# A two-layer diffusion trunk on one core: a new order for the opening's small products, and layer 1's spectrum products held in program order

## The chip, the core and the metric

The kernel runs on one NeuronCore of a Trainium2 chip. The metric is the device time of one execution in microseconds (us). Five engines work side by side, each with its own instruction stream: TensorE multiplies matrices (PE in the profile, PEld for its weight loads), VectorE (DVE) and ScalarE (ACT) work element by element, GpSimd (POOL) does a few small operations, and SyncE's queue (SP) issues the transfers from memory. Engines wait for one another through semaphores.

## The reference

Two layers (DEPTH = 2) over 256 context tokens and 256 latent tokens of width 1024. Each layer normalises, modulates with a vector that comes from `c` and `c_ctx` through `w_mod`, projects with `w_in`, runs four mixers (attention, a Hyena long convolution, pooling, gated MLP), gates and merges them, and ends with a SwiGLU block:

```python
mod = (act_lat @ w_mod[l] + b_mod[l])[:, None, :]
sh1, s1, g1, sh2, s2, g2 = jnp.split(mod, 6, axis=-1)
p = modulate(x, norm1_w[l], sh1, s1) @ w_in[l]      # rms_norm(x) * (1 + s1) + sh1
x = x + g1 * parallel_mixers(p, attn, lp)
x = x + g2 * swiglu(modulate(x, norm2_w[l], sh2, s2), ...)
```

The Hyena mixer needs filters that come from a small sine network (three layers of `sin(freq * (h @ w + b))`) and their spectra, which the kernel computes as products with a DFT matrix. All of it is float32.

## The kernel before

Everything is kept with features on the partitions: x is eight tiles of 128 features by 512 tokens. A weight unit of 128x1024 is fetched by SP, rounded to `whi` (ScalarE) and its remainder `wlo` (VectorE); activations are split the same way (`hh`, `hl`), and each product is three matmuls, hi·hi, hi·lo and lo·hi (`mm3`).

**The opening** (lines 654 to 758) stands inside `tc.manual_schedule()`: there each engine runs its instructions in the order in which the code writes them. It does the following.

- Eight tiles of x come in, then the weights of the modulation in four "chunks" (`w_mod`, eight transfers each), with a unit of `w_wide` behind each chunk.
- `dense(n)` issues products of ones that nobody reads, into the bank `warm`.
- The sums of squares: ScalarE squares each tile of x (line 678), and a product ones x squares adds it into all 128 rows of a bank (line 686, two records each in the profile, as float32 takes two passes). Tiles 4 to 7 are first added in pairs on VectorE (line 685).
- The diagonal of that bank is read by four reductions on VectorE (line 690), GpSimd raises it to the power -0.5 (line 695), `rstd_diag` spreads it over a diagonal (line 350, tile `dg`), and `rstd_spread` makes `rb`, the factor in all rows, by one product with ones (line 360).
- `chunk_mods(8)` multiplies one chunk (line 283, 64 records); its tail on VectorE is a transpose (line 294), additions (line 299) and the factor `amod` (line 304). Group g of two tiles of x needs chunk g.
- Four groups g = 0 to 3 follow. Each normalises tiles 2g and 2g+1 (`norm_tiles`: `nt` at line 382 begins the group, `hh` and `hl` of the first tile, then line 378, 389, 391 and 405 for the second), multiplies the first tile (`next(w0)`, line 728, twelve matmuls), does a step of the sine network, multiplies chunk g+1, and multiplies the second tile (twelve matmuls).
- `mlp` is the sine network, a generator in seven steps. Step 1 is the first product and three VectorE operations ("A", lines 414 to 417), step 2 the range reduction ("B", four operations, lines 420 to 422), step 3 the sine on ScalarE (line 424), the second product (line 434) and its A, step 4 its B, step 5 sine, third product and A, step 6 B, step 7 the last sine. Before, steps 1 and 2 stand ahead of the sums, step 3 within them, and steps 4 to 7 in the groups 0 to 3, each between the first tile's product and the next chunk's.

**After the opening** a planner orders each engine's instructions by what its own model says is ready; a wait on the chip follows from that order. `tc.keep_in_program_order(r)` binds an instruction behind the one that the code wrote just before it on its engine.

**The end of layer 0** is such a planned place. The last residual gives sums of squares, by columns: `sums_of` (line 322) multiplies 128 token columns of the squares, as weights, with one column of ones, four products (eight records, line 328) for a tile. `rstd` (one VectorE operation, line 337, and GpSimd's power, line 339) and `rstd_bcast` (lines 350 and 360) follow, and then layer 1's first tile. The code writes layer 1's spectrum products (`spectrum_mm`, five of six matmuls each, B0, B1, A0, A1, C0) around this chain: B0 behind the first `sums_of`, B1 and A0 behind the second, A1 and C0 behind the product that makes `rb`. The same pattern stands in the middle of layer 0 with the four filter products of layer 1 (`filter_mm`, line 474): the first behind the first `sums_of`, the second behind the chain's start, the third behind `rb`.

Of the kernel before, what the change touches and what calls it, by code (L numbers as in the profile page):

```python
# [11 lines left out]
F32 = mybir.dt.float32  # L12
# [3 lines left out]
ALU = mybir.AluOpType  # L16
AX = mybir.AxisListType

P = 128
D = 1024  # L20
KT = D // P
# [9 lines left out]
EPS = 1e-6  # L31
# [71 lines left out]
def trunk_kernel(ctx: ExitStack, tc: tile.TileContext, I, out: bass.AP):  # L103
# [32 lines left out]
    def load_const(name, shape):  # L136
        t = const(name, shape)
        SY.dma_start(out=t, in_=I[name])
        return t

    def split(hi, lo, src):
        S.copy(hi, src)
        V.tensor_sub(lo, src, f32(hi))
# [63 lines left out]
            split_next()  # L207
        flush()

    def mm3(o, wh, wl, xh, xl, first, last):  # L210
        T.matmul(o, lhsT=wh, rhs=xh, start=first, stop=False)  # L211
        T.matmul(o, lhsT=wh, rhs=xl, start=False, stop=False)  # L212
        T.matmul(o, lhsT=wl, rhs=xh, start=False, stop=last)  # L213


    pa = load_const("pack_a", [P, 280])
# [254 lines left out]
    def filter_mm(l, p, o):  # L471
        w3, _, f = flt[l]
        f[p, o] = side("pf")
        T.matmul(f[p, o], lhsT=hk[:, p * P : p * P + P], rhs=w3[o], start=True, stop=True)

    def filter_keep(l, p, o):

# [74 lines left out]
    def spectrum_mm(l, name, parts, fwd, nyq):  # L552

        k, col, mat = {
            "A0": (0, 0, fwd), "A1": (0, 128, fwd), "B0": (1, 0, nyq), "B1": (1, 384, fwd), "C0": (0, 128, nyq)
        }[name]
        o = side("sp")
        for p in range(2):
            h, lo = mat[p]
            mm3(o, h[:, col : col + P], lo[:, col : col + P], *parts[k][p], p == 0, p == 1)  # L560
        spectra.setdefault(l, {})[name] = o

    def spectrum_out(l, name, skip):
# [87 lines left out]
        return vec  # L651


    start = [True]
    opened = ExitStack()
    opened.enter_context(tc.manual_schedule())
    x = fresh_x()
# [6 lines left out]
    wide = t2(s="wide")  # L664
    V.memset(wide, 1.0)

    def dense(n):

        for _ in range(n):
            T.matmul(warm, lhsT=ones, rhs=wide, start=True, stop=True)  # L670

    dense(2)
    next(mlp)
# [2 lines left out]
    for j in range(KT):  # L676
        sq = t2(s="sq")
        S.activation(sq, x[j], AF.Square)
        if j == 3:
            next(mlp)  # L680
        if j in (4, 6):
            held = sq
            continue
        if j in (5, 7):
            V.tensor_add(sq, held, sq)
        T.matmul(tot, lhsT=ones, rhs=sq, start=(j == 0), stop=(j == KT - 1))
    r = small([P, 4], F32, "rs")
    for t in range(4):
        sl = slice(t * P, t * P + P)
        V.tensor_tensor_reduce(  # L690
            out=junk[:, :P], in0=tot[:, sl], in1=ident, scale=1.0 / D, scalar=EPS,
            op0=ALU.mult, op1=ALU.add, accum_out=r[:, t : t + 1],
        )
    r2 = small([P, 4], F32, "rs")
    G.tensor_tensor(r2, r, halfexp[:, :4], op=ALU.pow)
    dense(1)
    dg = rstd_diag(r2, 0, NTOK)
    chunk_mods(KT)
    rb = rstd_spread(dg, 0, NTOK)
    chunk_load(2)  # L700
    rest = []
    split_next(rest)
# [1 line left out]
    for l in range(DEPTH):  # L704
# [9 lines left out]
        def wide_gen(w, tset, ncols):  # L714
            os_ = {t: bank("w") for t in tset}
            for u in range(4):
                hi, lo = unit("w_wide", l, w, u)
                for k in range(2):
                    kt = 2 * u + k
                    hh, hl = hs[kt]  # L720
                    terms = [(hh, hi), (hh, lo), (hl, hi)]
                    ts = [(t, i) for t in tset for i in range(3)]
                    if start and kt % 2 == 0:
                        ts.sort(key=lambda v: v[1])
                    for t, i in ts:
                        n = ncols(t)
                        a, b = terms[i]
                        T.matmul(  # L728
                            os_[t][:, :n], lhsT=a[:, t * P : t * P + P], rhs=b[:, k * 512 : k * 512 + n],
                            start=(kt == 0 and i == 0), stop=(kt == 7 and i == 2),  # L730
                        )
                    if k:
                        done()
                    yield os_

        w0 = wide_gen(0, range(4), lambda t: 512 if t in tts else 256)
        if l == 0:
            def between(after):
                if not after and rest:
                    rest.pop(0)()  # L740

            for g in range(4):
                if g == 0:
                    chunk_load(3)
                if g:
                    split_next(rest)
                if g == 3:
                    SY.dma_start(out=pb[:, 646:], in_=I["pack_b"][:, 646:])
                    vec = vec_load(0)
                    silu_rows()  # L750
                hs += norm_tiles(l, 0, x, rb, 0, NTOK, range(2 * g, 2 * g + 2), between)
                if g == 3:
                    count["look"] = LOOK
                os_ = next(w0)
                next(mlp, None)
                chunk_mods(KT)
                os_ = next(w0)
            opened.close()
            start.clear()
        else:  # L760
            for i, h in enumerate(norm_tiles(l, 0, x, rb, 0, NTOK, range(KT))):
                hs.append(h)
                os_ = next(w0)
                if i in (2, 3, 4):
                    spectrum_out(1, ("A0", "A1", "C0")[i - 2], flt[1][3])
# [820 lines left out]
```

## Time and profile before

| what | value |
|---|---|
| time, median of 3 runs | 1321.97 us (1321.88 to 1325.45) |
| the profiled execution: its time | 1321.89 us |
| the profiled execution: its span, first to last instruction | 1320.1 us |
| matmuls of the span | 7694, TensorE busy 1293.7 us |
| mean granted TensorE clock | 0.997 of full speed |

1.79 us of the profiled time lie outside the span. Times in the rows are microseconds from the span's start. In a timeline row the columns are start, duration, engine, line, operation, tiles written and read, how many instructions were merged, and in brackets the idle time before them and what ended it.

### The profile page before, as it was taken

The numbers are of one execution on the slowest core, as the hardware profiler recorded it, in microseconds if no ns is written. First come the engines' busy times: TensorE is split into PE (matmuls) and PEld (weight loads), VectorE is DVE, ScalarE is ACT, GpSimd is POOL, SyncE is SP. The second block draws the span as 40 slices with busy tenths as digits, with TensorE's granted clock in tenths as the row PEclk, the third lists the DMA queues.
The fourth block names the chain that finished last, engine by engine and source line by source line (L and its number), as shares of the span: only waits on it lengthen the run. The fifth ranks groups of instructions, "written<-read, shape, count | busy, mean of one in ns | idle before, by whom it ended". The sixth has DMA issues, their size and how long they took to land.

```text
span 1320.1 us, 19990 instructions
## 1 busy us (share of the span) xinstructions
PE 1293.7 (98%) x7694; PEld 1121.6 (85%) x7694; DVE 936.7 (71%) x1615; ACT 607.6 (46%) x1059; POOL 64.1 (5%) x69
## 2 busy tenths in 40 slices
PE   8999999999999999999999999999999999999997
PEld 4778788888888878888888887889989999999997
DVE  5785896998977455677667677865889876655554
ACT  4652333377743336222122224365458854643443
POOL 0102300300000000000000000002110000000000
PEclk9999999999999999999999999999999999999999
DMA  9732234433445452554555553424434457565551
GB/s 352 284 100 92 88 120 139 134 127 105 131 137 170 157 184 97 159 176 159 170 168 178 186 176 128 159 80 129 140 106 139 151 191 251 160 185 183 184 185 48
DMA packets 68351, 204.90 MB, mean 155 GB/s; under 512 B 7584, under 2 KB 13856, under 8 KB 68128
## 3 DMA queue, kind: packets, MB, share of 16 engines
q1 hardware_dynamic: 68256, 203.63, 47.4%
q8 instruction: 60, 0.98, 0.3%
q14 instruction: 35, 0.29, 0.1%
HBM read 202.55 MB, written 1.05 MB: 154 GB/s over the span
## 4 chain that ended last, share of the span: by engine, by line
PE 72%; issue 17%; DVE 7%; ACT 2%; POOL 1%; DMA 0%; DVEq 0%; POOLq 0%; ACTq 0%
PE pmn L211 14%; PE pmn L213 14%; PE pmn L212 14%; PE pmw L728 4%; PE pmd L213 3%; PE pmd L212 3%; PE pmd L211 3%; PE pmb L211 2%; PE pmb L213 2%; PE pmb L212 2%; DVE wlo L176 2%; PE psav L1246 1%; PE pspt L1224 1%; PE pmk L211 1%; PE pmk L212 1%
## 5 line engine op out<-in xcount | busy, mean ns | idle before, releaser
L173 ACT CAST whi<-raw 128x1024 fp32r<-128x1024 f32 (+2 forms) x316 | 288.4, 920 | 476.2 <-PE pmn L212 221.0
L211 PE MATMUL pmn<-hh,whi 128*128 128x512 f32 (+1 forms) x1328 | 450.5, 339 | 0.6 <-DVE vst L777 0.6
L212 PE MATMUL pmn<-hl,whi 128*128 128x512 f32 (+1 forms) x1328 | 447.8, 337 | 0.0
L213 PE MATMUL pmn<-hh,wlo 128*128 128x512 f32 (+1 forms) x1328 | 446.7, 336 | 0.3 <-DVE wlo L176 0.3
L176 DVE TENSOR_TENSOR wlo<-raw,whi 128x1024 fp32r<-128x1024 f32 (+2 forms) x316 | 336.3, 1067 | 148.5 <-ACT whi L173 146.1
L211 PEld LDWEIGHTS pmn<-hh,whi 128*128 128x128 f32 x1328 | 251.9, 190 | 28.1 <-issue 1.1
L213 PEld LDWEIGHTS pmn<-hh,wlo 128*128 128x128 f32 x1328 | 251.8, 190 | 26.9 <-DVE wlo L176 0.7
L212 PEld LDWEIGHTS pmn<-hl,whi 128*128 128x128 f32 x1328 | 252.0, 190 | 26.5 <-issue 1.2
L253 DVE CUSTOM_DVE_ANT_0 junk<-raw,cb,pack_a 128x1024 bf16<-128x1024 f32 x144 | 187.1, 1299 | 1.4
L211 PE MATMUL pmd<-hh,whi 128*128 128x512 f32 (+1 forms) x352 | 118.8, 337 | 0.0
L212 PE MATMUL pmd<-hl,whi 128*128 128x512 f32 (+1 forms) x352 | 118.7, 337 | 0.0
L213 PE MATMUL pmd<-hh,wlo 128*128 128x512 f32 (+1 forms) x352 | 118.4, 337 | 0.0
L213 PEld LDWEIGHTS pmd<-hh,wlo 128*128 128x128 f32 x352 | 66.8, 190 | 7.2 <-issue 0.5
L212 PEld LDWEIGHTS pmd<-hl,whi 128*128 128x128 f32 x352 | 66.8, 190 | 7.1 <-issue 0.2
L211 PEld LDWEIGHTS pmd<-hh,whi 128*128 128x128 f32 x352 | 66.8, 190 | 7.1 <-issue 0.2
L1372 DVE TENSOR_TENSOR sg<-sg,pmn 128x512 f32<-128x512 f32 (+1 forms) x42 | 23.3, 554 | 64.9 <-PE pmn L213 64.9
L339 POOL TENSOR_TENSOR rs<-rs,halfexp 128x4 f32<-128x4 f32 (+1 forms) x4 | 3.4, 852 | 939.3 <-DVE rs L337 939.3
L728 PE MATMUL pmw<-whi,hh 128*128 128x512 f32 (+1 forms) x112 | 41.2, 386 | 2.5 <-ACT hh L385 1.4
L728 PE MATMUL pmw<-wlo,hh 128*128 128x512 f32 (+1 forms) x112 | 40.1, 376 | 0.0
L728 PE MATMUL pmw<-whi,hl 128*128 128x512 f32 (+1 forms) x112 | 39.9, 377 | 0.0
L1300 DVE SCALAR_TENSOR_TENSOR x<-pmd,mod,x 128x256 f32<-128x256 f32 x48 | 21.8, 478 | 24.5 <-PE pmd L213 24.5
L1209 ACT ACTIVATE pe<-pssc,mx 128x512 f32<-128x512 f32 (+1 forms) x48 | 29.6, 618 | 16.6 <-DVE mx L1206 16.5
(284 smaller groups left out, 1868.3 us busy)
## 6 DMA issues: line engine op xcount, KB each, us to landing
raw<-in_w_ff SPq DMA_DIRECT2D x88, 512.0 KB, 4.3
raw<-in_w_nar SPq DMA_DIRECT2D x84, 512.0 KB, 3.6
raw<-in_w_t SPq DMA_DIRECT2D x72, 512.0 KB, 3.7
raw<-in_w_dn SPq DMA_DIRECT2D x44, 512.0 KB, 4.1
raw<-in_w_mod SPq DMA_DIRECT2D x48, 256.0 KB, 5.9
raw<-in_w_wide SPq DMA_DIRECT2D x16, 512.0 KB, 3.6
raw<-in_w_out SPq DMA_DIRECT2D x16, 512.0 KB, 3.9
raw<-in_w_br SPq DMA_DIRECT2D x48, 128.0 KB, 2.1
```

Of the source, the lines that this page charges most:

```text
L173: S.copy(hi[:, c0:c1], raw[:, c0:c1])
L176: V.tensor_sub(lo[:, c0:c1], raw[:, c0:c1], f32(hi[:, c0:c1]))
L211: T.matmul(o, lhsT=wh, rhs=xh, start=first, stop=False)
L212: T.matmul(o, lhsT=wh, rhs=xl, start=False, stop=False)
L213: T.matmul(o, lhsT=wl, rhs=xh, start=False, stop=last)
L253: r = V.tensor_tensor_reduce(out=junk, in0=raw, in1=cb[:, s, :], scale=1.0, scalar=bmod[:, l, i : i + 1], op0=ALU.mult, op1=ALU.add, accum ...
L728: T.matmul(os_[t][:, :n], lhsT=a[:, t * P : t * P + P], rhs=b[:, k * 512 : k * 512 + n], start=(kt == 0 and i == 0), stop=(kt == 7 and i = ...
L1209: S.activation(e[:, :nk], sc[:, :nk], AF.Exp, bias=mx, scale=1.0, accum_out=den)
L1224: T.transpose(pt[:, k * P : k * P + P], e[:, k * P : k * P + P], ident)
L1246: T.matmul(av[:, b * 256 : b * 256 + 256], lhsT=vst[:, k, g, :], rhs=part[k // 2][:, (k % 2) * 256 : (k % 2) * 256 + 256], start=(k == 0 a ...
L1300: V.scalar_tensor_tensor(x[j][:, sl], o[:, sl], mod[l][:, gi * 8 + j, k : k + 1], x[j][:, sl], op0=ALU.mult, op1=ALU.add)
L1372: V.tensor_mul(sg[:, CS], sg[:, CS], o[:, CS])
```

## The change

Six edits in the opening and one outside of it.

1. The sums of squares go by columns: for each tile `sums_of` replaces the product of 512 columns; the pair additions are gone; behind tiles 0 to 4 stands an unread product of 256 columns.
2. `rstd` and `rstd_bcast` replace the four diagonal reads and the opening's own power; step 3 of the sine network stands behind `rstd`, and chunk 0 is multiplied in two halves, before and behind the product that makes `rb`.
3. Unread products of 512 and 256 columns follow the second half.
4. `wide_gen` hands over control once more in the middle of a unit's second tile, after six of its twelve matmuls, and the chunk is multiplied there.
5. The sine steps stand elsewhere: step 4 behind group 0's `norm_tiles`, step 5 behind group 1's chunk, step 6 behind group 3's `norm_tiles`, step 7 behind the groups.
6. `start` moves up, for `pin`.
7. `pin` keeps layer 1's spectrum products and filter products in program order on TensorE.

```diff
+    def pin(r):
+        if not start:
+            tc.keep_in_program_order(r)
+
+    start = [True]
...
-    def mm3(o, wh, wl, xh, xl, first, last):
-        T.matmul(o, lhsT=wh, rhs=xh, start=first, stop=False)
-        T.matmul(o, lhsT=wh, rhs=xl, start=False, stop=False)
-        T.matmul(o, lhsT=wl, rhs=xh, start=False, stop=last)
+    def mm3(o, wh, wl, xh, xl, first, last, held=False):
+        for i, (w, v) in enumerate(((wh, xh), (wh, xl), (wl, xh))):
+            r = T.matmul(o, lhsT=w, rhs=v, start=first and i == 0, stop=last and i == 2)
+            if held:
+                pin(r)
...
-        T.matmul(f[p, o], lhsT=hk[:, p * P : p * P + P], rhs=w3[o], start=True, stop=True)
+        r = T.matmul(f[p, o], lhsT=hk[:, p * P : p * P + P], rhs=w3[o], start=True, stop=True)
+        if l:
+            pin(r)
...
-            mm3(o, h[:, col : col + P], lo[:, col : col + P], *parts[k][p], p == 0, p == 1)
+            mm3(o, h[:, col : col + P], lo[:, col : col + P], *parts[k][p], p == 0, p == 1, l == 1)
...
-    def dense(n):
+    def dense(n, cols=512):
 
         for _ in range(n):
-            T.matmul(warm, lhsT=ones, rhs=wide, start=True, stop=True)
+            T.matmul(warm[:, :cols], lhsT=ones, rhs=wide[:, :cols], start=True, stop=True)
...
         S.activation(sq, x[j], AF.Square)
-        if j == 3:
-            next(mlp)
-        if j in (4, 6):
-            held = sq
-            continue
-        if j in (5, 7):
-            V.tensor_add(sq, held, sq)
-        T.matmul(tot, lhsT=ones, rhs=sq, start=(j == 0), stop=(j == KT - 1))
...
-    r2 = small([P, 4], F32, "rs")
-    G.tensor_tensor(r2, r, halfexp[:, :4], op=ALU.pow)
+        sums_of(tot, sq, 0, NTOK, j == 0, j == KT - 1)
+        if j < 5:
+            dense(1, 256)
+    r2 = rstd(tot, 0, NTOK)
+    next(mlp)
+    chunk_mods(4)
+    rb = rstd_bcast(r2, 0, NTOK)
+    chunk_mods(4)
     dense(1)
-    dg = rstd_diag(r2, 0, NTOK)
-    chunk_mods(KT)
-    rb = rstd_spread(dg, 0, NTOK)
+    dense(1, 256)
...
-                    for t, i in ts:
+                    for m, (t, i) in enumerate(ts):
+                        if start and k and m == len(ts) // 2:
+                            yield os_
...
+                if g in (0, 3):
+                    next(mlp)
                 if g == 3:
                     count["look"] = LOOK
                 os_ = next(w0)
-                next(mlp, None)
+                os_ = next(w0)
                 chunk_mods(KT)
+                if g == 1:
+                    next(mlp)
                 os_ = next(w0)
+            next(mlp, None)
```

## Rows read from the trace of the kernel before

**Rows 1.** The page's busy time of each engine, share of the span, instructions.

```profile
PE 1293.7 (98%) x7694; PEld 1121.6 (85%) x7694; DVE 936.7 (71%) x1615; ACT 607.6 (46%) x1059; POOL 64.1 (5%) x69
```

**Rows 2.** Windows of 25 us: busy time per engine, granted clock, DMA share, GB/s.

```profile
0.00:25.00 25.00, 20.50 (x168) 10.85 (x169) 13.43 (x40) 10.27 (x18) 1.77 (x6) 1.00 0.95 342
...
575.00:600.00 25.00, 25.00 (x112) 20.71 (x111) 17.91 (x26) 7.56 (x10) 0.00 (x0) 1.00 0.53 168
...
850.00:875.00 25.00, 22.93 (x106) 18.60 (x106) 14.13 (x24) 11.39 (x19) 1.01 (x1) 0.93 0.31 105
```

**Rows 3.** Timeline of the opening, up to group 0's first operation.

```profile
7.12 2.74 PE L686 MATMUL pmss<-sq,ones 128*128 128x512 f32 x6
...
9.69 0.68 PE L434 MATMUL psf<-sr,pack_b 128*128 128x256 f32 x2
...
11.32 0.29 DVE L417 TENSOR_SCALAR sk<-sk 128x256 f32<-128x256 f32 x1
...
12.27 1.98 PE L686 MATMUL pmss<-sq,ones 128*128 128x512 f32 x4 [1.04 <-DVE sq L685]
...
15.67 1.01 POOL L695 TENSOR_TENSOR rs<-rs,halfexp 128x4 f32<-128x4 f32 x1 [14.39 <-DVE rs L690]
...
17.46 1.13 PE L360 MATMUL psrb<-dg,ones 128*128 128x512 f32 x2 [0.47 <-DVE dg L350]
...
18.63 0.87 DVE L382 SCALAR_TENSOR_TENSOR nt<-x,amod,psrb 128x256 f32<-128x256 f32 x2 [0.60 <-PE psrb L360]
```

**Rows 4.** Timeline of the opening's groups: chunk 1, group 0's second tile, next groups' starts.

```profile
22.69 1.95 PE L283 MATMUL psmod<-raw,csf 128*32 128x128 f32 x64
...
23.88 0.69 DVE L405 TENSOR_TENSOR hl<-nh,hh 128x512 fp32r<-128x512 f32 x1 [1.26 <-ACT hh L391]
...
26.07 0.31 DVE L294 STREAM_TRANSPOSE modt<-psmod 128x128 f32<-128x128 f32 x1
...
26.81 0.87 DVE L382 SCALAR_TENSOR_TENSOR nt<-x,amod,psrb 128x256 f32<-128x256 f32 x2
...
43.94 0.87 DVE L382 SCALAR_TENSOR_TENSOR nt<-x,amod,psrb 128x256 f32<-128x256 f32 x2
```

**Rows 5.** Timeline of the opening's end: step 6 of the sines, first narrow unit.

```profile
41.62 1.34 DVE L420 SCALAR_TENSOR_TENSOR sa<-sk,sa 128x256 f32<-128x256 f32 x3
...
50.56 2.36 DVE L176 TENSOR_TENSOR wlo<-raw,whi 128x1024 fp32r<-128x1024 f32 x2 [0.56 <-ACT whi L173]
...
53.18 0.50 PE L211 MATMUL pmn<-hh,whi 128*128 128x512 f32 x1 [0.57 <-DVE vst L777]
```

**Rows 6.** Timeline of the middle of layer 0: sums by columns, layer 1's filter products.

```profile
485.67 1.96 PE L474 MATMUL pspf<-w,hyh 128*128 128x512 f32 x4
...
485.97 0.63 ACT L320 ACTIVATE sq<-x 128x512 f32<-128x512 f32 x1
...
487.47 0.95 PE L328 MATMUL pmss<-ones,sq 128*128 128x1 f32 x8
...
490.48 1.12 PE L360 MATMUL psrb<-dg,ones 128*128 128x512 f32 x2 [0.86 <-DVE dg L350]
...
493.12 0.95 PE L211 MATMUL pmk<-hh,whi 128*128 128x512 f32 x3 [0.51 <-ACT hh L385]
```

**Rows 7.** Timeline of ScalarE: casts of the weights of groups 1 and 3.

```profile
25.80 1.14 ACT L173 CAST whi<-raw 128x512 fp32r<-128x512 f32 x2 [1.95 <-DMA raw<-in_w_wide]
...
40.88 1.14 ACT L173 CAST whi<-raw 128x512 fp32r<-128x512 f32 x2
```

**Rows 8.** Timeline of the end of layer 0: VectorE behind, first spectrum product.

```profile
842.45 0.50 PE L211 MATMUL pssp<-fh,dh 128*128 128x512 f32 x1 [0.59 <-ACT fh L142]
...
843.73 3.49 DVE L176 TENSOR_TENSOR wlo<-raw,whi 128x1024 fp32r<-128x1024 f32 x3
```

**Rows 9.** Windows cut at the idle stretch there; columns as in rows 2.

```profile
863.51:865.57 2.06, 0.00 (x0) 0.00 (x0) 0.85 (x2) 0.00 (x0) 1.01 (x1) 1.00 0.68 245
865.57:868.98 3.41, 3.41 (x6) 2.10 (x7) 1.29 (x4) 0.78 (x2) 0.00 (x0) 0.50 0.02 6
```

More of the change, by code (lines that the diff above doesn't have):

```diff
@@ L651, in vec_load @@
         return vec
-    start = [True]
     opened = ExitStack()
@@ L678, in trunk_kernel @@
         S.activation(sq, x[j], AF.Square)
-        if j == 3:
-            next(mlp)
-        if j in (4, 6):
-            held = sq
-            continue
-        if j in (5, 7):
-            V.tensor_add(sq, held, sq)
-        T.matmul(tot, lhsT=ones, rhs=sq, start=(j == 0), stop=(j == KT - 1))
[L687 to L693, printed above, removed]
-    r2 = small([P, 4], F32, "rs")
-    G.tensor_tensor(r2, r, halfexp[:, :4], op=ALU.pow)
+        sums_of(tot, sq, 0, NTOK, j == 0, j == KT - 1)
[6 more added lines that the diff above has]
+    chunk_mods(4)
     dense(1)
-    dg = rstd_diag(r2, 0, NTOK)
-    chunk_mods(KT)
-    rb = rstd_spread(dg, 0, NTOK)
+    dense(1, 256)
     chunk_load(2)
```

## The prediction, as put on record before the change was run

> **What bounds the kernel now.** I read the page first: TensorE is busy for 1293.7 of 1320.1 us, 98% of the span [rows 1], so the kernel is one long stream of matmuls, and a change can only pay or cost where that stream stands still or where matmuls are added. Windows of 25 us over the whole span show where it stands still. Nearly all are full; the first has 4.5 us without a matmul and the one around 862 us has 2.1 us and a mean clock of 0.93 [rows 2]. Those are the two places that the change touches. So the timelines come next: the opening, engine by engine, to see which operation starts each group late, and the end of layer 0. The chain of waits was of no more use, since it is mostly the stream itself. A full window holds 112 matmuls of 512 columns in 25 us, 0.22 us each [rows 2].
>
> In the opening everything hangs on a chain: sums of squares, power, `rb`, and then each group's `nt`. Group 0's `nt` starts at 18.63 [rows 3], group 3's at 43.94 [rows 4], and the first narrow unit's matmul at 53.18 [rows 5], from where the stream is full. Whatever moves that matmul moves the end.
>
> **The sums of squares.** Before, a tile costs a product of 512 columns: six records in 2.74 us, 0.9 us for the two of one product [rows 3]. Six products and two additions follow the arrival of x and end at 14.25. After, every tile is eight one-column records. They are in the trace further on: 0.95 us for eight [rows 6], of which a little overlaps the next instruction, so 0.9. The five unread products of 256 columns are half of 0.9 each, 0.45. Eight times 0.9 and five times 0.45 are 9.45 us, and they can start where the sums start now, at 7.12. They end at 16.6. The squares are there earlier, so TensorE sets the pace.
>
> A rule of the Trainium skill speaks against this price. The page TensorE: Matmul & The Clock Gate, section Back-to-back issue gap, gives some 25 ns from start to start for 1 to 64 moving columns; by it eight records take 0.2 us and the sums would end with the last square. The row says 0.12 us a record, as each brings its own 128 columns of weights, so I keep 0.9.
>
> **From the sums to group 0.** In the middle of layer 0, the same helpers take 2.06 us from the end of the sums (487.47 + 0.95 = 488.42) to `rb`'s product at 490.48 [rows 6]. Here step 3 of the sines comes between: its product stands behind the sums, and its three VectorE operations stand ahead of `dg`. From the start of such a product (9.69) to the end of the third operation (11.32 + 0.29) are 1.92 us, and from the end of the power (15.67 + 1.01 = 16.68) to `rb` (17.46) 0.78 for `dg` [rows 3]. So `rb` starts at 16.6 + 1.92 + 0.78 = 19.3, against 17.46. The second half of chunk 0 now follows it on TensorE: 0.95 for `rb`'s two records and half of a chunk's 1.95 us. Then the chunk's tail, 0.74 from transpose to `nt` (26.07 to 26.81), and some 0.06 before it [rows 4]. Group 0 starts at 19.3 + 0.95 + 0.98 + 0.8 = 22.0, 3.4 us later. The diagonal reads that go away (14.25 to 15.67) are already counted in this.
>
> **The groups.** Call the start of `nt` T. Before, TensorE multiplies chunk 1 (22.69, T + 4.1) while ScalarE and VectorE still make the second tile: `hh` is there at 23.85 (T + 5.2) and `hl` at 24.57 (T + 5.9) [rows 4]. The chunk fills that hole. After, the second tile's first six matmuls stand ahead of the chunk, in token order, so the third of them needs `hl`. TensorE waits from T + 4.1 to T + 5.25, starts the third at T + 5.95, ends the sixth at T + 7.1, ends the chunk at T + 9.05, and with 0.8 for the tail the next `nt` is at T + 9.85. Three such periods are 29.55. In group 1 step 5's product follows the chunk, and its A stands on VectorE ahead of the next `nt`: 1.92 from the product's start, T + 10.97, 1.1 more. Together 30.7. Before, three periods are 43.94 - 18.63 = 25.3, the delays by the sine steps included. So group 3 starts 3.4 + 5.4 = 8.8 us later.
>
> The weights don't set this pace. Group 1's cast waited 1.95 us for its transfer, but group 3's at 40.88 waited for nothing [rows 7], and every group now starts later.
>
> **The end of the opening.** Step 6 (1.34 us and a fourth operation of 0.29) moves from a place where it delayed chunk 3's tail to behind the last `hl`. There VectorE waits 0.56 us for a cast, then makes two `wlo` and after them the `vst` for which the narrow unit's bank waits [rows 5]. 1.63 - 0.56 = 1.07 us comes on top, unless the planner, which may reorder what follows the opening, puts `vst` earlier; the bounds are 0 and 1.07. I take 1.0. The opening: 8.8 + 1.0 = **+9.8 us**. Its bounds: without step 5's 1.1 and the last 1.0, +7.7; with 1.08 for a tile's sums instead of 0.9, +11.2.
>
> **Layer 1's filter products.** Before, the planner put two of them (0.86 each) ahead of the last sums, which start at 487.47 although the squares are there at 486.60 (485.97 + 0.63). Pinned, the second goes behind the sums and fills the wait for `rb` instead, where TensorE has 0.86 us idle [rows 6]. The chain starts 0.8 earlier, and the wait at 493.12 with it: **-0.8 us**, bounds 0 and -0.8.
>
> **Layer 1's spectrum products.** Before, the first of the thirty run from 842.45, after 0.59 us idle, as fillers while `wlo` is late on VectorE [rows 8]. Then nothing is left for the wait for `rb`: 2.06 us idle, and behind it the granted clock is 0.50, the lower of the two levels (1.2 GHz), for 3.41 us, in which work that takes half of it is done [rows 9]. Pinned, B1 and A0 (twelve matmuls of 0.22, 2.7 us) stand in the wait and fill it. If the planner finds other products for the hole at 842, all three losses go: 0.59 + 2.06 + 1.7 = 4.35. If it doesn't, TensorE waits there until the first of three `wlo`, a third of the 3.49 us from 843.73, at 844.9; from 841.86, where the idle time now begins, that is 3.0 instead of 0.59, and the gain is 4.35 - 2.4 = 1.95. The `hi` products of that unit and of the next ones need no `wlo`, but the planner stopped using them before, so I take the middle, **-3.1 us**.
>
> **The sum**, against the profiled execution's own 1321.89 (1320.1 of span and 1.79 around it, 0.08 under the median of the runs): +9.8 - 0.8 - 3.1 = +5.9, 1327.8 us. With the bounds: +7.7 - 0.8 - 4.35 is 1324.4, and +11.2 - 0 - 1.95 is 1331.1. Differences under 0.3% (4 us) can't be told from no change.
>
> **Rivals.**
> - *The weights set the pace of the groups*, so that the opening's new order costs nothing; what is left is -3.9, 1318.0, not slower. For it: the DMA engines are 95% busy in the first window [rows 2], and group 1's cast waited. Against it: group 3's cast didn't. It decides only if group 3's weights land later than its new `nt` at 52.7. Chance 0.13.
> - *The sums cost less*: TensorE follows the squares, the sums end no later than 14.25, and the opening costs 2.3 less: 1325.5. For it speaks only that the squares are early, against it the 0.95 us. Chance 0.13. By the 25 ns of the Trainium skill's page the sums would end before 12.3, where the trace now begins the pairs' products, and the time would be some 1323.5.
> - *The clock falls in the opening.* One-column records and waits take the place of wide products, and the trace shows it fall behind sums by columns and 2.06 us of idle [rows 9]. Each such stretch costs 1.7: one or two give 1329.5 to 1331.2. Against it: unread products stand between, and the longest new wait is 1.2 us. Chance 0.11.
> - *The pins don't help*: the planner fills the hole at 842 with nothing, and late `wlo` later give the rest back. Then the opening stands alone: 1331.7. Chance 0.13.
>
> **How the numbers follow.** The forecast as it stands has 0.50, with a range of its own from 1324.4 to 1331.1. Slower by over 0.3% (above 1325.9): 0.40 of it, the clock and the pins whole, and a little of the cheap sums: 0.65. Within 0.3%: the rest of it, most of the cheap sums, and half of the weights' case: 0.27. Faster: half of the weights' case, and what I overlooked: 0.08. The range for 8 in 10 is 1321.5 to 1333: it leaves out the weights' case and the far ends of the others.
>
> **What would show it.** In the changed profile: the last sums' record near 16.5; group 0's `nt` near 22, group 3's near 52.7, each chunk behind an idle stretch of 1.2 us; the first narrow matmul near 63; no idle stretch before `rb` at the end of layer 0, and no clock of 0.50 there. The prediction is wrong if the periods of the groups stay near 8.2, or if the sums end before 15; then the opening is no loss and layer 1 alone decides.

## The result, and the profile after

The changed kernel takes 1338.55 us (median of four runs, 1335.67 to 1343.3), against 1322.86 for the kernel before: a ratio of 1.0116, interval 1.0099 to 1.0133. It is slower by 15.7 us, outside the range of 1321.5 to 1333. The profiled execution is the quickest of the four, 1335.67 us, 13.8 over the profiled one of before.

The page of the changed kernel, its line of busy time, answers to [rows 1]; the windows under it to [rows 2]:

```profile
PE 1305.6 (98%) x7758; PEld 1131.0 (85%) x7758; DVE 934.5 (70%) x1606; ACT 608.1 (46%) x1059; POOL 63.4 (5%) x69
```

```profile
0.00:25.00 25.00, 23.04 (x154) 15.61 (x154) 6.93 (x22) 8.18 (x14) 1.77 (x6) 0.86 0.93 335
...
850.00:875.00 25.00, 21.85 (x91) 17.57 (x90) 16.81 (x24) 6.71 (x10) 0.00 (x0) 0.93 0.48 156
```

TensorE is "busier" than before in the first window (23.0 against 20.5 us) and does less there: the granted clock is 0.86 where it was 1.00. The window at 862 keeps its clock of 0.93, which the pins were to raise.

**The opening**, timeline up to group 0's `nt`, against [rows 3]:

```profile
7.25 0.95 PE L335 MATMUL pmss<-ones,sq 128*128 128x1 f32 x8
...
13.88 3.17 PE L335 MATMUL pmss<-ones,sq 128*128 128x1 f32 x24
...
16.91 1.20 PE L441 MATMUL psf<-sr,pack_b 128*128 128x256 f32 x2
...
20.00 2.08 PE L367 MATMUL psrb<-dg,ones 128*128 128x512 f32 x2
...
22.01 1.46 PE L290 MATMUL psmod<-raw,csf 128*32 128x128 f32 x32
...
24.29 0.88 DVE L389 SCALAR_TENSOR_TENSOR nt<-x,amod,psrb 128x256 f32<-128x256 f32 x2
```

Windows of the same kernel, cut where the clock changes (columns as in rows 2):

```profile
6.00:16.00 10.00, 10.00 (x74) 8.98 (x73) 2.70 (x7) 4.72 (x8) 0.00 (x0) 1.00 1.02 375
16.00:22.83 6.83, 6.80 (x58) 4.05 (x61) 1.90 (x5) 1.14 (x2) 1.01 (x1) 0.50 1.04 390
22.83:40.00 17.17, 14.19 (x130) 9.35 (x122) 11.91 (x30) 6.91 (x14) 0.00 (x0) 1.00 1.04 394
```

While the last sums run, the clock falls to the lower level (1.2 GHz) for 6.83 us, with no idle time ahead of it: TensorE was busy for all 10.00 us of the window before. In that stretch lies most of what the prediction calls the path: the sines' product takes 1.20 us in place of 0.68, `rb` 2.08 in place of 1.13, and the second half chunk, in which the clock rises again, 1.46 in place of the 0.98 forecast. `nt` starts at 24.29, 5.66 us later than before, where 3.4 were forecast.

**The groups and the end of the opening**, timeline, against [rows 4, 5]:

```profile
29.57 0.50 PE L727 MATMUL pmw<-whi,hh 128*128 128x512 f32 x1 [1.14 <-ACT hh L398]
...
31.43 1.95 PE L290 MATMUL psmod<-raw,csf 128*32 128x128 f32 x64
...
34.21 0.87 DVE L389 SCALAR_TENSOR_TENSOR nt<-x,amod,psrb 128x256 f32<-128x256 f32 x2
...
55.21 0.87 DVE L389 SCALAR_TENSOR_TENSOR nt<-x,amod,psrb 128x256 f32<-128x256 f32 x2
...
61.07 1.34 DVE L427 SCALAR_TENSOR_TENSOR sa<-sk,sa 128x256 f32<-128x256 f32 x3
...
62.65 2.35 DVE L182 TENSOR_TENSOR wlo<-raw,whi 128x1024 fp32r<-128x1024 f32 x2
...
65.26 0.50 PE L218 MATMUL pmn<-hh,whi 128*128 128x512 f32 x1 [1.48 <-DVE vst L781]
```

The hole ahead of the second tile (1.14 us, released by `hh`) is no longer filled; from `nt` to `nt` it is 9.92 us, and over the three periods 30.92 against 25.31. From group 3's `nt` to the first narrow matmul it is 10.05 against 9.24. That matmul starts 12.1 us later than before.

**Layer 1's pins.** Middle of layer 0, timeline, against [rows 6]:

```profile
500.35 1.05 PE L335 MATMUL pmss<-ones,sq 128*128 128x1 f32 x8
...
501.26 1.10 PE L481 MATMUL pspf<-w,hyh 128*128 128x512 f32 x2
...
503.47 1.12 PE L367 MATMUL psrb<-dg,ones 128*128 128x512 f32 x2
...
506.11 0.96 PE L218 MATMUL pmk<-hh,whi 128*128 128x512 f32 x3 [0.50 <-ACT hh L392]
```

The filter product now stands in the wait, and `rb` has no idle time ahead of it. End of layer 0, timeline and windows, against [rows 8, 9]:

```profile
856.84 2.35 DVE L182 TENSOR_TENSOR wlo<-raw,whi 128x1024 fp32r<-128x1024 f32 x2
858.11 0.50 PE L218 MATMUL pmd<-hh,wlo 128*128 128x512 f32 x1 [3.15 <-DVE wlo L182]
...
880.73 1.02 PE L367 MATMUL psrb<-dg,ones 128*128 128x512 f32 x2
```

```profile
169.60:173.02 3.42, 3.42 (x9) 2.68 (x10) 3.16 (x8) 1.21 (x5) 0.81 (x1) 0.50 0.17 46
854.96:858.11 3.15, 0.00 (x0) 0.00 (x1) 3.09 (x5) 1.06 (x3) 0.00 (x0) 1.00 0.31 118
...
859.10:862.51 3.41, 3.41 (x9) 2.64 (x9) 3.16 (x6) 0.63 (x1) 0.00 (x0) 0.50 0.94 288
```

The wait for `rb` is filled and its half clock gone, as forecast. But the hole that the spectrum products used to fill is 3.15 us of nothing, with 3.41 us at half clock behind it: idle time and lost clock have moved, not gone. The first window is new too: at 169.6 us the clock falls behind 1.52 us of idle time that the kernel before has as well (ahead of its 156.6), there without a fall.

The sum of the trace, read from how far the same instructions lie apart in the two traces: +12.1 at the first narrow matmul, +1.6 at 169 us, -0.7 in the middle of layer 0, +0.1 near 810 us, +0.3 at the end of layer 0, +0.4 in the middle of layer 1, in all +13.8. The last is not explained by any run here.

### The profile page after: what moved, and what is told of

Its sections match the earlier page's. It is cut to its first block, busy times and chain, and to the rows that moved or that the text cites. A ratio compares the mean times of both kernels' runs of the same rounds, so it can differ in the third digit from the quotient of the medians.

```text
span 1333.9 us, 20107 instructions
## 1 busy us (share of the span) xinstructions
PE 1305.6 (98%) x7758; PEld 1131.0 (85%) x7758; DVE 934.5 (70%) x1606; ACT 608.1 (46%) x1059; POOL 63.4 (5%) x69
## 4 chain that ended last, share of the span: by engine, by line
PE 72%; issue 16%; DVE 6%; DMA 2%; ACT 2%; POOL 1%; SPq 0%; POOLq 0%; DVEq 0%; ACTq 0%
PE pmn L218 42%; PE pmd L218 8%; PE pmb L218 5%; PE pmw L727 4%; PE pmk L218 3%; DVE wlo L182 1%; PE psav L1250 1%; PE pspt L1228 1%; DMA raw<-in_w_mod 1%; PE psiv L218 1%; PE pssp L218 1%; PE pssc L1207 1%; PE pssc L1208 1%; PE psU L218 1%; PE psmod L290 1%
## 5 line engine op out<-in xcount | busy, mean ns | idle before, releaser
L218 PEld LDWEIGHTS pmn<-hl,whi 128*128 128x128 f32 x1328 | 252.3, 190 | 26.8 <-issue 1.2
L218 PEld LDWEIGHTS pmd<-hh,wlo 128*128 128x128 f32 x352 | 67.1, 191 | 10.9 <-DVE wlo L182 3.6
```

The costliest lines, as they stand in the source:

```text
L218: r = T.matmul(o, lhsT=w, rhs=v, start=first and i == 0, stop=last and i == 2)
```

## The experiments

**Each pin and each half of the opening by itself** (e1 to e3), and the changed kernel again (e4).

e1: `before` with `pin` in `filter_mm` and `mm3(..., held=l == 1)` in `spectrum_mm`; the opening is that of before.

> The kernel before with the two kinds of pins alone (edits 6 and 7); the opening is the old one. Theory 1 (as the trace of the changed kernel reads): the filter pins give 0.75 us, and the spectrum pins give nothing, because the hole at the end of layer 0 stays empty (about 3.1 us of idle time in place of 0.6) and has a stretch of half clock of its own (1.7 us lost), which takes the place of the wait and the half clock before rb's product. Time 0.5 to 1 us under the kernel before. Rival (the prediction): the half clock in the hole belongs to the changed kernel's other timing, and without the new opening the pins give 3 to 4 us, near 1318 to 1319.

Measured: 1322.2 us against 1323.27, ratio 0.9994 (0.9986 to 1.0003). In the trace, windows of e1:

```profile
841.98:845.13 3.15, 0.00 (x0) 0.00 (x0) 3.08 (x5) 1.06 (x3) 0.00 (x0) 1.00 0.29 112
845.70:849.11 3.41, 3.41 (x10) 2.67 (x9) 2.84 (x5) 0.63 (x1) 0.00 (x0) 0.50 0.80 241
```

The same hole and half clock stand there with the old opening. Against the trace of before, the middle of layer 0 is 0.6 us shorter with the filter pins, and from the last `pstot` of layer 0 to layer 1's first product the spectrum pins cost 0.3. Theory 1's mechanism held, though its 0.5 to 1 us can't be told from nothing by the times; the rival's 3 to 4 us are not there.

e2 is `before` with edits 1 to 3, e3 `before` with edits 4 and 5; one place of each (cut):

```diff
+        sums_of(tot, sq, 0, NTOK, j == 0, j == KT - 1)
+        if j < 5:
+            dense(1, 256)
...
+                        if start and k and m == len(ts) // 2:
+                            yield os_
```

> The kernel before with edits 1 to 3 alone: sums of squares by columns with unread products, step 3 of the sines moved, chunk 0 in two halves; the groups run as before. Theory 1 (the clock falls because of the column sums): granted clock 0.50 from about 15.6 us on for some 7 us, group 0's nt at 24.3 and the first narrow matmul at about 58.9, 5.7 us later than before, time near 1327.6 or 1.7 more if the clock falls again at 169 us. Rival A (the prediction's price without a fall of the clock): nt at 22.0, first narrow matmul at 56.6, time near 1325.3. Rival B (the groups are paced by the weights): nt late but the first narrow matmul within 2 us of 53.2.

Measured: 1332.54 us, from 1330.29 to 1336.85, ratio 1.0075 (1.0055 to 1.0096). Timeline of e2:

```profile
12.67 1.71 PE L328 MATMUL pmss<-ones,sq 128*128 128x1 f32 x8
...
27.37 0.87 DVE L382 SCALAR_TENSOR_TENSOR nt<-x,amod,psrb 128x256 f32<-128x256 f32 x2
```

In the traced run (1334.78) the clock is at half from 12.05 to 25.70 us, `nt` starts at 27.37, and from there to the first narrow matmul it is 34.47 us against 34.55 before: the groups don't take back anything (rival B falls), and rival A's 22.0 isn't reached. Theory 1's mechanism is right, its 24.3 too low: the clock fell earlier than in the changed kernel's trace.

> The kernel before with edits 4 and 5 alone: the chunk in the midst of the second tile, sine steps 4 to 7 moved; sums and rb as before. Theory 1: the new group periods of 9.9, 11.0 and 10.0 us (25.3 to 30.8 in all) and about 1 us at the end of the opening, first narrow matmul near 59.6, no stretch of half clock in the opening, time near 1328.3, up to 1.7 more if the clock falls at 169 us here too. Rival A: the waits of 1.2 us in every group let the clock fall, and the group periods are 1 to 2 us longer. Rival B: group 0 starts early enough that the weights' transfers pace the groups and the periods differ from those of the changed kernel.

Measured: 1330.67 us (1329.05 to 1330.92), ratio 1.0058 (1.0043 to 1.0073). First and last `nt` and the first narrow matmul of e3:

```profile
19.06 0.87 DVE L382 SCALAR_TENSOR_TENSOR nt<-x,amod,psrb 128x256 f32<-128x256 f32 x2 [0.60 <-PE psrb L360]
...
49.70 0.87 DVE L382 SCALAR_TENSOR_TENSOR nt<-x,amod,psrb 128x256 f32<-128x256 f32 x2
...
59.75 0.51 PE L211 MATMUL pmn<-hh,whi 128*128 128x512 f32 x1 [1.46 <-DVE vst L784]
```

30.64 us for the periods and 10.05 to the end, near the 30.92 and 10.05 of the changed kernel, though group 0 starts only 0.43 us later than before and the clock is 1.00 throughout the groups: theory 1.

Against the median of before in the same series (1323.27 us) the three parts are worth -1.1, +9.3 and +7.4 us, together +15.6; the changed kernel was 15.7 slower at first and 18.0 in e4.

> The changed kernel itself, unaltered: its four runs so far lie at 1336 and at 1341 to 1343 us, and only one at 1336 has a trace. Theory 1: the two groups of times are two ways in which the clock falls or does not fall at the same places, and they differ by 5 to 7 us in a single stretch of the span; a trace of a run near 1342 would show where. Rival: times are spread evenly between 1335 and 1344, and no single place explains it. Expected times: some runs near 1336, some near 1342.

Measured: 1341.22 us, six runs at 1335.95, 1337.71, 1339.0, 1343.45, 1344.28 and 1344.61. The traced one (1344.28) has its place in the opening, timeline of e4:

```profile
8.61 1.71 PE L335 MATMUL pmss<-ones,sq 128*128 128x1 f32 x8
...
10.18 1.20 PE L678 MATMUL pmw<-wide,ones 128*128 128x256 f32 x2
...
21.41 5.12 PE L335 MATMUL pmss<-ones,sq 128*128 128x1 f32 x24
...
29.48 2.07 PE L367 MATMUL psrb<-dg,ones 128*128 128x512 f32 x2
...
33.46 0.87 DVE L389 SCALAR_TENSOR_TENSOR nt<-x,amod,psrb 128x256 f32<-128x256 f32 x2
```

Eight records take 1.71 us where they took 0.95, the 256 columns 1.20 in place of 0.68: all at half clock from the start. The first record of the clock in this trace, a rise, stands at 31.7 us (5.8 in the other); where there is none yet, the windows print 1.00, which is why the slower run shows the higher mean clock. `nt` is 9.2 us later than in the other trace, the span 8.6 longer. So the single place of theory 1 is found, with more than its 5 to 7 us, but the times between (1337.71, 1339.0) show more than two ways.

**What in the opening holds the clock down** (e6 to e8, from the changed kernel). e6 puts the wide sums back:

```diff
-        sums_of(tot, sq, 0, NTOK, j == 0, j == KT - 1)
-        if j < 5:
-            dense(1, 256)
-    r2 = rstd(tot, 0, NTOK)
+        if j in (4, 6):
...
+        T.matmul(tot, lhsT=ones, rhs=sq, start=(j == 0), stop=(j == KT - 1))
...
+    G.tensor_tensor(r2, r, halfexp[:, :4], op=ALU.pow)
```

> The changed kernel with edit 1 undone: sums of squares as products of 512 columns with the pair additions and the four diagonal reads, no unread products between; everything else of the change stays. Theory 1 (the column sums let the clock fall in the opening, and in some runs it doesn't rise before 31.7 us): the granted clock is 1.00 from about 6 us on in every run, group 0's nt is near 20.4 in place of 24.3, the first narrow matmul near 61.4 in place of 65.3, the times lie close together near 1331.8 (1330.1 if the clock doesn't fall at 169 us either) and no run is near 1342. Rival: something else of the opening sets the clock (the halves of the chunk, step 3 of the sines, the wait for power and dg), and half clock or two groups of times stay.

Measured: 1330.1 us (1329.54 to 1330.88), ratio 1.0052 (1.0039 to 1.0065), one group of times. Timeline of e6, and its windows at the hole:

```profile
13.03 1.13 PE L692 MATMUL pmss<-sq,ones 128*128 128x512 f32 x2 [0.23 <-DVE sq L691]
...
17.42 1.12 PE L367 MATMUL psrb<-dg,ones 128*128 128x512 f32 x2 [1.83 <-DVE dg L357]
...
20.37 0.87 DVE L389 SCALAR_TENSOR_TENSOR nt<-x,amod,psrb 128x256 f32<-128x256 f32 x2
...
61.06 0.50 PE L218 MATMUL pmn<-hh,whi 128*128 128x512 f32 x1 [1.49 <-DVE vst L792]
```

```profile
850.79:853.94 3.15, 0.00 (x1) 0.01 (x1) 3.09 (x5) 1.05 (x3) 0.00 (x0) 1.00 0.27 107
853.94:857.00 3.06, 3.06 (x13) 2.54 (x14) 2.90 (x4) 0.63 (x1) 0.00 (x0) 1.00 0.70 187
```

Theory 1 held: with wide sums the opening has no half clock behind the first rise, and `rb` stands where it stood before (17.46). What is left is the second half of the chunk behind it (1.7 us) and the groups (6.1). Between the medians of the changed kernel and of e6 edit 1 thus costs 8.45 us, and 11.1 by the six runs of e4. In the hole the same 3.15 us of idle time are here not followed by a fall of the clock, and the stretch around the end of layer 0 is 1.3 us shorter than before.

e7 leaves out the five unread products (`if j < 5: dense(1, 256)`), e8 puts `dense(1, 512)` behind every tile in their place.

> The changed kernel without the five unread products of 256 columns between the sums. Theory 1 (the column sums themselves keep the clock down and the unread products are too little to hold it up): half clock in most of the opening in all runs, a tile's sums take 1.7 us in place of 0.95, times near those of the changed kernel, 1336 to 1342. Rival (the prediction's price with the clock at 1.00): eight times 0.95 from 7.25 us, the sums end at 14.9, nt at 20.3, first narrow matmul near 61.3, time near 1331.7.

Measured: 1336.54 us (1332.8 to 1341.25), ratio 1.0102 (1.0082 to 1.0123). All 64 records of e7:

```profile
7.23 11.91 PE L335 MATMUL pmss<-ones,sq 128*128 128x1 f32 x64
```

Half clock from 9.13 to 22.78 us, `nt` at 25.36: theory 1, though two of the four runs are quicker than its 1336. At the full level eight times 0.95 would be 7.6. The times overlap those of the changed kernel (1335.67 to 1344.61), so what the five products of 256 columns do to the time is not shown.

> The changed kernel with an unread product of 512 columns behind every tile's sums in place of the five of 256. Theory 1 (the unread work was too small): the clock stays at 1.00 in every run, the sums with their unread products take 0.9 + 0.9 per tile from 7.25 us and end at 20.7, a last unread product stands ahead of the sines' product, nt near 27, first narrow matmul near 68, time near 1338 with no second group of times. Rival: the clock falls or doesn't rise in spite of them, sums and unread products take up to twice as long, nt near 33 to 40 and the time 1344 to 1351 in such runs.

Measured: 1351.29 us (1351.19 to 1351.84), ratio 1.0213 (1.0199 to 1.0226). Timeline of e8:

```profile
8.61 1.71 PE L335 MATMUL pmss<-ones,sq 128*128 128x1 f32 x8
10.17 2.05 PE L678 MATMUL pmw<-wide,ones 128*128 128x512 f32 x2
...
32.50 1.71 PE L335 MATMUL pmss<-ones,sq 128*128 128x1 f32 x8
...
38.87 1.13 PE L367 MATMUL psrb<-dg,ones 128*128 128x512 f32 x2 [0.43 <-DVE dg L357]
```

The rival, and worse than its bounds (`nt` at 41.81): from 8.6 us to behind the last sums everything runs at the lower level, nearly twice as long, and the first record of a rise is at 37.9, although TensorE was busy from 5.6 us on without a pause. More unread work between the sums didn't help; it was paid for at half clock.

**The two edits of the groups apart** (e9): `before` with the `yield` and a second `os_ = next(w0)` ahead of `chunk_mods(KT)`, the sine steps where they were.

> The kernel before with edit 4 alone: the chunk in the midst of the second tile, every sine step still right behind the first tile's products. Theory 1 (the prediction's split of the groups): the token order behind the third matmul costs 4.3 us over three periods, and the sine steps' new places (edit 5) cost the rest of the 6.6 us of the run with edits 4 and 5 together; the third product of the sines now delays the second tile of group 1 by some 0.6 us, so the first narrow matmul stands near 57.5 to 58.2 against 53.18 and the time near 1326.5. Rival: the new place of the chunk alone costs everything, first narrow matmul near 59.7.

Measured: 1329.45 us (1328.65 to 1329.89), ratio 1.004 (1.0027 to 1.0052). The clock rises late in the traced run (10.0 us) and `nt` is 2.1 us later than before for that alone. Timeline of e9:

```profile
20.75 0.87 DVE L382 SCALAR_TENSOR_TENSOR nt<-x,amod,psrb 128x256 f32<-128x256 f32 x2 [0.60 <-PE psrb L360]
...
50.90 0.87 DVE L382 SCALAR_TENSOR_TENSOR nt<-x,amod,psrb 128x256 f32<-128x256 f32 x2
...
60.03 0.50 PE L211 MATMUL pmn<-hh,whi 128*128 128x512 f32 x1 [0.57 <-DVE vst L780]
```

From `nt` on it is 30.15 + 9.13 = 39.28 us against 34.55: edit 4 alone costs 4.7, and edit 5 the rest, 0.5 in the periods and 0.9 at the end (e3). The first narrow matmul stands where the rival had it, but 2.1 us of that lie ahead of group 0; without them it is 57.9, as in theory 1. The period of group 1 is 10.33 us where the other two are 9.91, 0.4 for the sines' product. The time is above theory 1's 1326.5 in all four runs, of which one has a trace.

**Can the spectrum products serve both places, and can the clock be made to rise?** e5 is e1 with `held=l == 1 and name in ("B1", "A0")`; e12 has the filter pins alone. e10 and e11 put four small products at the start of the changed kernel and of the kernel before (with the filter pins); e16 is e11 with the second wide product cut to 256 columns.

```diff
+    for _ in range(4):
+        T.matmul(warm[:, :P], lhsT=ones, rhs=ones, start=True, stop=True)
     dense(2)
```

> The kernel before with the filter pins and, of the spectrum products, only B1 and A0 pinned; B0, A1 and C0 stay free. Theory 1 (the spectrum pins failed only because they take the filler out of the hole at 842 us): B0's six matmuls run in the hole again (1.35 us), so its idle time falls from 3.15 to about 1.8 us (0.6 ahead of B0 and 1.2 behind it) and the clock stays up there; B1 and A0 fill the wait for rb as before, with no idle and no half clock behind it. Against the kernel before: 2.06 + 1.7 less, 1.2 more, and 0.75 less for the filter pins, in all 3.3 us, near 1320. Rival: 1.2 us of idle so close behind another 0.6 us lets the clock fall all the same, or the planner leaves the hole empty: 0.5 to 1.6 us under the kernel before.

Measured: 1323.32 us against 1323.75, ratio 1.0000 (0.9990 to 1.0010). B0 fills the hole as theory 1 has it (0.60, 0.32 and 0.30 us of idle left in the trace), but TensorE then stands 0.91 us ahead of the last sums, and the clock falls 1.3 us after B1 and A0 begin to fill the wait: from the hole to layer 1's first product it takes 28.46 us against 28.48 before. Theory 1's 3.3 us are not there: nearer the rival, though by another path, and its 0.5 us aren't shown either.

> The kernel before with the filter pins alone. Theory 1 (the term of the prediction): the idle stretch of 0.86 us before rb in the middle of layer 0 is gone, everything behind it starts 0.75 us earlier, and the end of layer 0 is as it was (0.59 us of idle at 842, 2.06 before rb). Time 0.7 us under the kernel before, near 1321.2 in its lower group of times. Rival: the shift moves the stretches of half clock, and 1.7 us more or less come on top.

Measured: 1323.75 us against 1323.76, ratio 0.9999 (0.9988 to 1.0010), runs from 1321.07 to 1326.74. In the trace (a run of 1326.5 with a rise at 10.9 us and half clock at 161 and 868 us) the middle of layer 0 is 0.65 us shorter. The 0.65 us stand in the rows but can't be seen in the times: a stretch of half clock more or less, as the rival has it, is worth more.

> The changed kernel with four more unread products of 128 columns (ones times ones) at the very start, so that TensorE works from about 1.05 us on instead of 1.88; nothing on the path to the end is added. Theory 1 (the runs near 1342 are those in which the clock doesn't rise before the sums by columns begin, and an earlier start of the engine makes it rise in time): all runs near 1336, none above 1338. Rival A: whether it rises has nothing to do with the 0.8 us, and two groups of times stay, 1336 and 1342. Rival B: all runs fall into the late group.

Measured: 1336.44 us (1333.52 to 1339.65), ratio 1.0093 (1.0076 to 1.0110). Six runs, none above 1340, where five of ten of the changed kernel are above 1341, too few to show that the late times are gone; two lie above theory 1's 1338. In the trace (1339.65) the clock rises at 6.3, no earlier than the 5.8 of the changed kernel, and is at half from 13.1 to 26.8. Theory 1 fell: a rise ahead of the sums isn't kept through them. The small products also push the sines' first product back, which the expectation left out.

> The kernel before with the filter pins and the same four early unread products. Theory 1: the filter pins give 0.75 us, and the early start makes the clock rise at about 5.5 us in every run, where the kernel before has runs near 1322 and runs near 1324 (a late rise of the clock); times near 1321 in all runs, 1 to 2 us under the median of the kernel before. Rival: no effect of the early start, 0.75 us under the kernel before with the same two groups.

Measured: 1322.7 us against 1323.76, ratio 0.9990 (0.9982 to 0.9999), runs from 1320.84 to 1323.75 where before has 1321.43 to 1325.86. Theory 1 is not borne out: only one of eleven runs is near 1321, and in the trace the clock rises at 7.2, not at 5.5.

> The kernel before with the filter pins and four unread products of 128 columns at the very start; to keep the first product of the sines at 5.6 us, the second of the two wide unread products behind them is cut to 256 columns. Theory 1: the early start makes the clock rise before 8 us in every run, and 0.9 us of e11's delay is gone: median near 1321.8, 1.5 to 2 us under the kernel before, no run above 1323. Rival: with less wide work ahead of 5.6 us the clock rises as late as it does in the kernel before, and runs of 1324 to 1326 stay.

Measured: 1322.13 us against 1322.07, ratio 0.9999 (0.9990 to 1.0009), with runs up to 1325.61. In its trace the clock rises at 6.2, but five runs lie above 1323: theory 1 fell, and e11's 0.1% is not repeated in this variant. No version here is shown to beat the kernel before by more than its own runs differ.

**Fewer records, or a warm start** (e13 to e15). e13 is e12's kernel, e14 the changed one, with

```diff
+        if j < KT - 2:
+            sumsq_add(x, acc, j, 0, NTOK)
...
+        if j >= KT - 3:
+            sums_of(tot, sq if j >= KT - 2 else acc, 0, NTOK, j == KT - 3, j == KT - 1)
```

and `dense(1)` behind the first three (e13) or four (e14) tiles; e15 has `dense(5)` in place of `dense(1)` ahead of the sums.

> The kernel before with the filter pins; in the opening the squares of tiles 0 to 5 are added on VectorE and only that sum and tiles 6 and 7 are summed by columns (24 records, no diagonal reads), three wide unread products stand where TensorE has nothing to do. Theory 1 (64 one-column records are what keeps the clock down; 24 behind wide work do not): no half clock between the rise and 60 us, rb near 15.6 against 17.46, first narrow matmul 1.5 to 2 us earlier, time 2 us or more under the kernel before. Rival A: the weights' transfers pace the groups, and rb is earlier but the first narrow matmul isn't. Rival B: 24 records are enough to let the clock fall, and the opening is slower than before.

Measured: 1329.33 us (1327.8 to 1330.16), ratio 1.0044 (1.0032 to 1.0057). Timeline of e13:

```profile
15.61 1.05 PE L334 MATMUL pmss<-ones,acc 128*128 128x1 f32 x8 [2.69 <-DVE acc L322]
16.52 2.47 PE L334 MATMUL pmss<-ones,sq 128*128 128x1 f32 x16
...
24.41 1.17 PE L366 MATMUL psrb<-dg,ones 128*128 128x512 f32 x2
```

Not foreseen: the additions queue on VectorE behind the sines and end at 15.6, where the old sums ended at 14.25. The clock rises late in this trace (10.9), and it is at half from 17.7 to 24.6 us, behind 2.69 us of idle time and 2.11 of one-column records. Rival B by its time; whether the records or the idle time let the clock fall, this run can't tell.

> The changed kernel with the same sums (24 one-column records in place of 64, four wide unread products). Theory 1: no half clock in the opening, group 0's nt near 19 against 24.3, first narrow matmul near 60, times in one group near 1329, like the run with wide sums or a little under. Rival: the new order (halves of the chunk around rb, step 3 of the sines) lets the clock fall by itself, and times of 1333 to 1342 stay.

Measured: 1331.22 us (1329.46 to 1334.49), ratio 1.0062 (1.0046 to 1.0079). Half clock for 3.4 us from 15.6, behind 2.30 us of idle; `nt` at 21.90. Between theory 1 and the rival: this opening, with fewer records and wider unread products, loses less.

> The changed kernel with five wide unread products in place of one ahead of the sums (3.6 us more of wide work). Theory 1 (a clock that has not risen when the sums by columns begin doesn't rise during them): in every run it rises before the sums, no run stays at half until after 30 us, and the times lie between 1335 and 1340 in spite of the 3.6 us; the clock still falls within the sums, as in the other traces. Rival: runs near 1345 and above remain, so that the rise does not depend on what stands ahead of the sums.

Measured: 1339.82 us (1336.49 to 1344.25), ratio 1.0126 (1.0101 to 1.0151). In the trace (1340.28) the clock rises at 10.3, ahead of the sums; they take 0.95 us a tile until it falls at 20.6, for 6.83 us. The trace agrees with theory 1, but two of the four runs lie above its 1340, and the one at 1344.25 has no trace and leaves it open whether the rise came in every run.

## Why the prediction was wrong

Two steps failed. In the profiled run, 7.9 us above the forecast, the opening has 2.3 of them and the spectrum pins 3.4; 2.1 came at places that the sum left out, 1.6 of these behind the 1.52 us wait. In the trace of e4, 16.5 us above it, the opening alone has 11.2.

- **From the sums to group 0**: the step that failed first. The price at the full clock was right: 1.33 us from tile to tile (7.25 to 8.58) for 1.35 forecast, the sums a little cheaper and the unread products a little dearer than forecast. The forecast of `nt` at 22.0 stood on that clock. It was at half in all nine traces with sums by columns in the opening (changed kernel, e2, e4, e7, e8, e10, e13 to e15), for 3.4 us or more; in all nine with wide sums it wasn't once it had risen (between 5.4 and 10.9 us). `nt` came 5.7 us late in one trace of the changed kernel and 14.8 in the other, in place of 3.4. Wide sums alone take 8.45 us back (e6).
- **The rival "the clock falls in the opening"** had the mechanism, at a chance of 0.11. "Unread products stand between" was no argument: the clock falls with them (changed kernel) and without them (e7), and with wider ones it doesn't rise before 37.9 us (the trace of e8). Its price of 1.7 for each of one or two stretches fits the profiled run, where `nt` is 2.3 later than forecast; but it supposed that the clock would rise as early as before, and in e4 it rose at 31.7. The measured 1338.55 is the middle of two runs near 1336 and two above 1341.
- **The groups**: right, for the reason given. 30.92 us against a forecast of 30.7 worked out from 1.2 us of idle time and the late `hl`, and 9.92, 10.96 and 10.04 us for its 9.85, 10.97 and 9.85. In all nine traces with edits 4 and 5 it is 30.6 to 30.9, whether group 0 starts at 19.06 (e3) or at 41.81 (e8), so the weights' rival fell.
- **The end of the opening**: +0.8 for a forecast of 1.0.
- **Filter pins**: right, -0.7 for -0.8 (0.6 in e1).
- **Spectrum pins**: the second step that failed; forecast -3.1, measured +0.3 (e1 and the changed kernel). The planner doesn't fill the hole: 3.15 us idle, as the lower bound had it (3.0). That bound left out a half clock of the hole's own, 1.7 us. It was also added up wrongly: its 4.35 already holds the 0.59 us of idle time, so 3.0 and not 2.4 had to be taken off, which leaves a gain of 1.35 in place of 1.95. Less 1.7 that is a loss of 0.35, close to the 0.3 measured; and where the clock stayed up behind the hole (e6 and e8) the pins gave 1.3.

**What stays open.** Why the same idle time is followed by a fall of the clock in one execution and not in the next: a fall stands behind the 1.52 us before `psiv` in eight of the eighteen traces, behind the 3.15 us of the hole in seven of nine, and within or behind the 2.06 us before `rb` in all eight that have them. Which property of the one-column records holds the clock down is not shown either, nor which order of work TensorE needs to rise and stay up during the sums. The runs show what it did, not how it decides. No run shows the weights setting the pace of the groups.

## What to carry to other kernels

Before a product is made cheap in columns, look at what it does to TensorE's clock where it stands: 64 one-column records cost their own time and then part of what follows them at half speed, and unread products between them didn't hold the clock up; the wide ones of e8 made it worse. A filler that is pinned into one hole leaves open the hole where the planner had used it; price both, with the clock behind each. And when a kernel's runs differ by more than 0.1%, take a trace from either end of the spread before pricing anything at a microsecond.

## What the runs showed of the hardware

- The rise of the clock at the start is not fixed: the first record of it stands at 5.4 to 10.9 us in the nine traces with wide sums. With sums by columns it stands at 5.2 to 10.9 in seven, each time ahead of the sums, and at 31.7 (e4) and 37.9 (e8) in the two where the sums had begun before a rise. The Trainium skill, TensorE: Matmul & The Clock Gate, says under What's actually happening that the number of slow matmuls at the start varies between runs of one kernel, and puts the loss under 1% of a typical span; the traces agree with both (8.6 us of 1342.5), but here it falls on the path.
- In none of the nine traces with sums by columns in the opening does the clock rise while these run, the first time or again; in e5, e9 and e12 it first rises within the wide sums (10.4, 10.0 and 10.9 us). In the changed kernel, e2, e7, e10 and e15 it falls during the sums by columns without any idle time since the rise: TensorE's busy time doesn't show it coming.
- A one-column record with its own weights takes 0.12 us (0.10 from the start of eight to the start of what follows); such a product is two records. The 25 ns that the Trainium skill's page TensorE: Matmul & The Clock Gate gives in its section Back-to-back issue gap don't hold for it. In its section LDWEIGHTS (loading the stationary operand) the same page of the Trainium skill gives the width of the weights over 1.2 GHz, an estimate of 0.107 us for 128 columns, and the rows at the full clock agree with that.
- At half clock these records take nearly twice as long as well (1.71 us for eight in place of 0.95), where weights and a single column are all that moves.
